# Products with the values as three float32r products of high and low parts, in one step of a hybrid GLA and attention backbone

## The chip, the cores and the metric

The kernel runs on one core of a Trainium2 chip, and the other cores are idle. A core has five engines, each with an instruction queue of its own that it works off in order: PE (TensorE, matrix products; the loading of its stationary operand is shown apart as PEld), DVE (VectorE), ACT (ScalarE), POOL (GpSimd) and SP (SyncE, which issues most transfers). They meet only through semaphores. SBUF is the on-chip memory; PE writes to PSUM, eight banks of 2 KB per partition, which DVE and ACT can read. The metric is the device time of one execution in microseconds; of several runs the median is given.

## The reference, cut to what matters

One inference step of two layers over 256 context tokens and 1024 latent tokens, model width 1024. Layer 0 mixes tokens with gated linear attention (GLA) of 4 heads, keys 128 wide and values 256 wide, scanned in both directions; layer 1 is grouped-query softmax attention. The change is in layer 0 alone:

```python
def step(S, inp):                       # one chunk of tokens, one head, one direction
    qi, ki, vi, gi = inp
    b = jnp.cumsum(gi, axis=2)
    b_last = b[:, :, -1:, :]
    qe = qi * jnp.exp(b)
    ke = ki * jnp.exp(-b)
    a = jnp.where(mask, jnp.einsum("bhtk,bhsk->bhts", qe, ke), 0.0)
    o = jnp.einsum("bhts,bhsv->bhtv", a, vi) + jnp.einsum("bhtk,bhkv->bhtv", qe, S)
    S = jnp.exp(b_last[:, :, 0, :])[..., None] * S + jnp.einsum(
        "bhsk,bhsv->bhkv", ki * jnp.exp(b_last - b), vi)
    return S, o
```

Two products have the values `vi` as an operand: the masked scores `a` times `vi` (the output inside a chunk), and the decayed keys transposed times `vi` (what a chunk adds to the state). All of it is in float32.

## The kernel before

The 1280 tokens are ten tiles of 128 (tiles 0 and 1 context, 2 to 9 latent). A start-up phase (to about 93 us) loads, normalises and modulates the tokens. Then comes the loop, `gla`, over five passes of ten tiles, 50 slots. In pass h (0 to 3) the tiles of head h go through decays, keys, scores and the scan in one direction; in pass h + 1 the other direction of head h is combined with it, scaled by its gate and stored. The fifth pass only combines. The same slots carry much other work as cover for each other: projections of the next heads (`mm3`, L247, each as three fp16 products of high and low halves), the splitting of attention weights into such halves (`split_ahead`, L329 and L330; `fill`, L308 and L309), and products with the conditioning vectors (L425). After the loop (about 540 us) follow the output projection of layer 0, the attention layer, and the last output projection.

In a slot, the parts that the change touches are these:

- `value_gate`: PE projects a tile's values into a PSUM bank (`mm`); ACT scales them into the SBUF tile `v` (L714, 128x256, three buffers).
- `intra`: PE transposes the decayed keys `en` of both directions into the bank `kt` (L781) and multiplies them with the queries `qe` into the other half of the bank (L784). DVE copies the transposed keys to `ks` (L787, 128x256) and masks the scores into `am` (L792); POOL adds the two directions to `at` (L793, 128x128).
- `outer`: PE multiplies `ks` with `v` for each direction into the bank `U` (L805 and L809), which ACT (L812) and DVE (L834) take into the scan; `scan` scales the state on POOL (L830, tiles `Sa`, `Sc`) and adds `U` on DVE (`Wa`, `Wc`).
- `local`: PE multiplies `at` with `v`, adds `qe` times the state in the same bank `A` (L851), and ACT copies it to `oa` (L854).

An fp32 product stands as one MATMUL in the program (it loads its own weights) and as two LDWEIGHTS and two MATMULs in the trace.

The order of the instructions on each engine is set when the kernel is built: a scheduler gives every instruction a priority in the order in which the code was written, shifted by the number that the table `LATER` has for the name of its `with self.later(name)` block (a higher number means later). Transfers from SP and ACT are set up by hardware; POOL's own (48 of them, most of them the attention outputs, L1408) use descriptors that POOL writes to a scratch in SBUF.

Of the kernel before, what the change touches and what calls it, by code (L numbers as in the profile page):

```python
# [9 lines left out]
F32 = mybir.dt.float32  # L10
I32 = mybir.dt.int32
AF = mybir.ActivationFunctionType
ALU = mybir.AluOpType
# [38 lines left out]
    "loc": -30,  # L52
    "kt": 30,
    "A": -110,
    "intra": -5,
    "ks": -90,
    "combine": -15,
    "cs": -40,
    "vg": -10,
    "u": 75,  # L60
    "gated": 50,
    "decay": -25,
    "outer": 10,
    "Uc": -100,
    "a9.qr": 30,
    "a.s1": 30,
    "gate": -5,
    "a0.key": -85,
    "x.qr": -40,
    "z.val": 35,  # L70
    "o": -155,
    "x.q": -15,
    "a0.qr": 15,
    "x.prep": -150,
    "oa": 30,
    "jobs": -20,
    "a.q": -210,
    "x.mod": -60,
    "x.res": -225,
    "a.val": 20,  # L80
    "a9.gate": 5,
    "a9.q": -200,
    "a.s0": -25,
    "a.qr": -200,
    "a9.s1": -160,
    "a0.s1": 390,
    "pieces8": 95,
    "filler": -30,
    "a0.s0": 75,
    "at": -115,  # L90
    "a0.rest": 30,
    "a0.gate": 65,
    "silu": -150,
    "a9.s0": -20,
    "x.setup": -150,
    "a9.val": 5,
    "combine9": 70,
    "jobs9": 220,
    "filler9": 15,
    "x.key8": 150,  # L100
    "eres": 110,
    "emod": -60,
    "wo2": 30,
    "fold": -30,
    "a0.q": 30,
    "wo3": 245,
    "x.key": -150,
    "s.v": 400,
    "s.q1": 60,
    "s.r0": -150,  # L110
    "s.n2": -55,
    "s.r1": 115,
    "gated9": 60,
    "eprep": 400,
    "x.kset": -30,
    "s.q0": -50,
    "s.s0": -140,
    "s.m1": -100,
    "s.s1": 220,
    "s.rk": 70,  # L120
    "s.n1": -100,
    "a9.val.3": -80,
    "a.s0.1": -15,
    "a9.val.1": -5,
    "a9.rest.0": 25,
    "a9.rest.2": -60,
    "a.rest.0": 100,
    "a.val.1": 25,
    "z.val.0": -100,
    "a.q.0": -110,  # L130
    "a9.qr.1": 60,
    "z.val.1": 165,
    "a9.gate.2": 85,
    "a9.s1.0": -200,
    "a9.q.0": -210,
    "a9.gate.0": -5,
    "a9.q.2": 30,
    "a9.s1.2": -135,
    "a.s0.3": -100,
    "a.s1.0": 55,  # L140
    "a9.gate.3": 15,
    "a9.s1.3": -150,
    "z.prep": -5,
    "a9.s0.0": -25,
}
# [15 lines left out]
class K:  # L161
# [545 lines left out]
    def value_gate(self, h, i, w):  # L707
        a, b = 0 if h < GH else DV, 2 * DV if h > 0 else DV
        ps = self.bank("mm")
        with self.later("vg"):  # L710
            self.tok_proj(i, [t[:, :, a:b] for t in w[0:2]], ps[:, a:b])
        if h < GH:
            v = self.t(self.tl, [P, DV], F32, "v", bufs=3)
            self.nc.scalar.activation(v, ps[:, 0:DV], AF.Copy, scale=self.inv_v[h])  # L714
            self.v[h][i] = v
        if h > 0:
            x = self.t(self.ew, [P, DV], F32, "gx", bufs=3)
            self.nc.scalar.activation(x, ps[:, DV:], AF.Copy, scale=self.inv_g[h - 1])  # L718
            with self.later("silu"):
                self.silu(x, DV)  # L720
            return x
# [49 lines left out]
    def intra(self, i, st):  # L771
# [13 lines left out]
        ks = self.t(self.ew, [P, 2, P], F32, "ks")  # L785
        with self.later("ks"):
            nc.vector.tensor_copy(ks, kt)  # L787
# [6 lines left out]
        st["at"], st["ks"] = at, ks  # L794


    def outer(self, h, i, a, st, prev, last):
# [5 lines left out]
        if needa:  # L803
            with self.later("Ua"):
                nc.tensor.matmul(ub[:, a, :], ks[:, a, :], v, start=True, stop=True)  # L805
        st["u"] = None
        if i < NTP or prev is not None:
            with self.later("Uc"):
                nc.tensor.matmul(ub[:, c, :], ks[:, c, :], v, start=True, stop=True)  # L809
# [33 lines left out]
    def local(self, h, i, a, st):  # L843
        nc = self.nc
        o = self.bank("A")[:, 0:DV]
        terms = [(st["at"], self.v[h][i])]
        if st["S"] is not None:
            terms.append((st["qe"][:, a, :], st["S"]))
        with self.later("local"):
            for j, (x, y) in enumerate(terms):  # L850
                nc.tensor.matmul(o, x, y, start=j == 0, stop=j == len(terms) - 1)  # L851
# [1103 lines left out]
```

## Time and profile before

| | |
|---|---|
| median of 3 runs | 1241.89 us (1240.9 to 1245.12) |
| profiled execution, span | 1240.9 us |
| PE busy | 1190.7 us (96%), 7990 MATMULs |
| DVE busy | 944.9 us (76%), 2177 instructions |
| ACT busy | 687.0 us (55%), 1694 instructions |
| POOL busy | 320.5 us (26%), 566 instructions |

The profiled execution is one run, and its own time is its span. A row of a group gives line, engine, operation, written tile, read tiles, shapes and count; then busy time, mean ns of one; then the idle time of the engine just before, and what ended it. A row of a line's own view gives minimum, median and maximum ns and the first and last start. A row of the timeline gives start, duration, engine, line and operation. A row of stages gives the stretch, its length, and for each engine busy us and (x instructions); then the granted clock of PE, the busy share of the DMA engines and GB/s.

### The profile page before, as it was taken

Reading aid. Unit: us, or ns where it says so; the run is one execution under the profiler, and the core shown is the slowest. Engines: PE = TensorE matmul, PEld = TensorE weight load, DVE = VectorE, ACT = ScalarE, POOL = GpSimd, SP = SyncE. Lnnn points to the kernel's source line nnn. Section 1 sums busy time; section 2 is a strip of 40 time slices with the busy share of each in tenths; the row PEclk is TensorE's granted clock in tenths of the full one; section 3 lists DMA queues with packets and bytes.
Section 4 is the critical chain, followed back from the end, with each engine's and each line's share of the span. In section 5 each row is a group of like instructions: output and inputs, shape, how many; then the busy total and the mean of one; then the engine's idle time right before and its main releaser. Section 6 shows DMA issues by size and latency. Waiting matters only on the chain. (4 is left out here: it accounts for less than half of the span.)

```text
span 1240.9 us, 22365 instructions
## 1 busy us (share of the span) xinstructions
PE 1190.7 (96%) x7990; PEld 778.3 (63%) x7990; DVE 944.9 (76%) x2177; ACT 687.0 (55%) x1694; POOL 320.5 (26%) x566
## 2 busy tenths in 40 slices
PE   5799999999999999799999999999999999989998
PEld 3467765655556566667776666776767666666444
DVE  4787779887888789976875787877767587786653
ACT  2565556665666657742333576666767676664110
POOL 0132122323321143311212443431322343311000
PEclk9999999999999999999999999999999999999999
DMA  9511566456555544489978787777958666979432
GB/s 378 196 69 73 196 202 228 127 185 203 175 191 164 189 132 161 112 186 307 204 174 203 178 163 138 132 145 133 199 124 161 124 118 132 205 139 246 158 137 85
DMA packets 318496, 210.14 MB, mean 169 GB/s; under 512 B 257158, under 2 KB 294702, under 8 KB 310064
## 3 DMA queue, kind: packets, MB, share of 16 engines
q1 hardware_dynamic: 311232, 191.18, 60.1%
q10 hardware_dynamic: 4688, 10.57, 2.2%
q0 software_dynamic: 2464, 6.95, 2.0%
q8 instruction: 63, 1.03, 0.3%
q14 instruction: 49, 0.40, 0.1%
HBM read 108.35 MB, written 38.96 MB: 119 GB/s over the span
## 5 line engine op out<-in xcount | busy, mean ns | idle before, releaser
L247 PEld LDWEIGHTS <-hT_hi 128*128 128x128 f16 x1920 | 187.6, 98 | 122.0 <-issue 5.6
L247 PE MATMUL mm<-whi,hT_hi 128*128 128x512 f16 (+1 forms) x576 | 200.2, 348 | 3.5 <-ACT gx L718 3.0
L247 PE MATMUL mm<-whi,hT_lo 128*128 128x512 f16 (+1 forms) x576 | 200.4, 348 | 0.0
L247 PE MATMUL mm<-wlo,hT_hi 128*128 128x512 f16 (+1 forms) x560 | 194.3, 347 | 0.7 <-DVE wlo L309 0.7
L247 PEld LDWEIGHTS <-whi 128*128 128x128 f16 x1232 | 120.3, 98 | 62.1 <-issue 2.2
L1344 PE MATMUL S<-kT,wst 128*128 128x512 f16 (+1 forms) x624 | 142.1, 341 | 4.1 <-ACT p L1352 4.0
L247 PE MATMUL mm<-hT_hi,whi 128*128 128x256 f16 (+1 forms) x480 | 141.1, 294 | 2.0 <-ACT gx L1392 2.0
L247 PE MATMUL mm<-hT_hi,wlo 128*128 128x256 f16 (+1 forms) x480 | 141.1, 294 | 0.0
L247 PE MATMUL mm<-hT_lo,whi 128*128 128x256 f16 (+1 forms) x480 | 141.1, 294 | 0.0
L1382 DVE SCALAR_TENSOR_TENSOR phl<-p,srec,phl 128x1280 f16<-128x1280 f32 (+1 forms) x79 | 105.3, 1332 | 40.6 <-ACT phl L1381 26.9
L247 PEld LDWEIGHTS <-hT_lo 128*128 128x128 f16 x960 | 94.1, 98 | 61.8 <-issue 1.1
L247 PE MATMUL mm<-PT,vh 128*128 128x256 f16 x672 | 114.6, 273 | 8.1 <-DMA PT<-phl 7.8
L1347 DVE TENSOR_REDUCE smx<-S 128x1 f32<-128x1280 f32 (+1 forms) x80 | 101.3, 1271 | 27.0 <-PE S L1344 26.9
L1352 ACT ACTIVATE p<-S,snb,acol 128x1280 f32<-128x1280 f32 (+1 forms) x80 | 99.1, 1239 | 12.5 <-DVE phl L1382 7.0
L1344 PEld LDWEIGHTS <-wst 128*128 128x128 f16 x624 | 61.4, 98 | 55.7 <-issue 6.9
L247 PE MATMUL mm<-PT,vl 128*128 128x256 f16 x336 | 91.6, 273 | 0.0
L1379 POOL TENSOR_SCALAR phl<-p,srec 128x1280 f16<-128x1280 f32 (+1 forms) x40 | 53.1, 1327 | 105.0 <-DVE srec L1370 57.1
L247 PEld LDWEIGHTS <-wlo 128*128 128x128 f16 x616 | 60.2, 98 | 29.2
L247 PEld LDWEIGHTS <-vh 128*128 128x128 f16 x672 | 65.1, 98 | 18.3 <-DMA PT<-phl 7.2
L1172 POOL TENSOR_TENSOR rope<-hx,ropet 128x64 f32<-128x64 f32 x160 | 51.2, 350 | 81.3 <-ACT hx L1308 63.8
L270 DVE TENSOR_REDUCE wmx<-wst 128x1 f32<-128x512 f32 x104 | 65.1, 677 | 3.5 <-DMA wst<-in_att_w 2.0
L238 POOL TENSOR_TENSOR hrs<-hrsa,mhalf 128x2 f32<-128x2 f32 x50 | 38.7, 775 | 106.8 <-DVE hrsa L236 106.5
(383 smaller groups left out, 2684.9 us busy)
## 6 DMA issues: line engine op xcount, KB each, us to landing
wada<-in_w_ada SPq DMA_DIRECT2D x16, 1024.0 KB, 5.4
wst<-in_att_w SPq DMA_DIRECT2D x14, 1024.0 KB, 5.3
wst<-in_gla_w_in SPq DMA_DIRECT2D x12, 1024.0 KB, 5.5
og_d<-og POOLq DMA_DIRECT2D x40, 128.0 KB, 2.8
wst<-og_d SPq DMA_DIRECT2D x5, 1024.0 KB, 6.0
og_d<-gx SPq DMA_DIRECT2D x37, 128.0 KB, 2.1
xr<-x_d SPq DMA_DIRECT2D x9, 512.0 KB, 3.3
out<-xr ACTq DMA_DIRECT2D x17, 256.0 KB, 2.0
```

Of the source, the lines that this page charges most:

```text
L238: nc.gpsimd.tensor_tensor(r, a, self.mhalf[:, 0:w], ALU.pow)
L247: self.pe = self.nc.tensor.matmul(out, a, b, start=k == 0 and j == 0, stop=k == n - 1 and j == 2).ins
L270: nc.vector.tensor_reduce(mx[:, j : j + 1], st[:, 2 * j : 2 * j + 2, :], AX.XY, ALU.max, apply_absolute_value=True)
L1172: nc.gpsimd.tensor_tensor(tv[:, h, :, w, :], xv[:, h, :, 1 - w, :], sn[:, :, w, :], ALU.mult)
L1344: nc.tensor.matmul(S[:, a : a + n], x, y, start=m == 0, stop=m == 2)
L1347: last = nc.vector.tensor_reduce(mx, S, AX.X, ALU.max).ins
L1352: nc.scalar.activation(p, S, AF.Exp, scale=self.sexp, bias=nb, accum_out=den)
L1379: nc.gpsimd.tensor_scalar(hi, p, r, 2.0 ** 14, ALU.mult, ALU.mult)
L1382: nc.vector.scalar_tensor_tensor(lo, p, r2, hi, ALU.mult, ALU.subtract)
```

## The change

`v`, the transposed keys and the masked scores are each kept as two float32r tiles: a high part, which is the value cast to float32r, and a low part, which is the value less its high part. A product with the values becomes three float32r products that add up in the same PSUM bank: high by high, high by low, low by high (`times_v`). The product of `qe` with the state stays one fp32 product. Per slot of passes 0 to 3 this adds on DVE the low part of `v` (`vlo`, 128x256) and the low part of the keys (`kl`, 128x256); the high part of the keys (`ks`) moves from a DVE copy to an ACT cast; ACT also gets the cast of `at` (128x128) and POOL its low part (128x128). The MATMULs written for these products go from 112 to 336. The scratch for POOL's descriptors shrinks from its default of 16384 bytes per partition to 4096. Nearly all numbers of `LATER` are new, and it has one new name, `vlo`.

```diff
+F32R = mybir.dt.float32r
 LATER = {
-    "kt": 30,
-    "A": -110,
-    "ks": -90,
+    "kt": 90,
+    "A": -265,
+    "ks": 110,
...
+    "vlo": 140,
 }
...
-            v = self.t(self.tl, [P, DV], F32, "v", bufs=3)
-            self.nc.scalar.activation(v, ps[:, 0:DV], AF.Copy, scale=self.inv_v[h])
-            self.v[h][i] = v
+            hi = self.t(self.tl, [P, DV], F32R, "v", bufs=3)
+            lo = self.t(self.tl, [P, DV], F32R, "vlo", bufs=3)
+            self.nc.scalar.activation(hi, ps[:, 0:DV], AF.Copy, scale=self.inv_v[h])
+            with self.later("vlo"):
+                self.nc.vector.scalar_tensor_tensor(
+                    lo, ps[:, 0:DV], self.inv_v[h], hi.bitcast(F32), ALU.mult, ALU.subtract
+                )
+            self.v[h][i] = hi, lo
...
-        ks = self.t(self.ew, [P, 2, P], F32, "ks")
+        ks = [self.t(self.ew, [P, 2, P], F32R, t) for t in ("ks", "kl")]
         with self.later("ks"):
-            nc.vector.tensor_copy(ks, kt)
+            nc.scalar.copy(ks[0], kt)
+            nc.vector.tensor_tensor(ks[1], kt, ks[0].bitcast(F32), ALU.subtract)
...
             nc.gpsimd.tensor_tensor(at, am[:, 0, :], am[:, 1, :], ALU.add)
-        st["at"], st["ks"] = at, ks
-
+            ah = [self.t(self.tl, [P, P], F32R, f"at{j}", bufs=2) for j in range(2)]
+            nc.scalar.copy(ah[0], at)
+            nc.gpsimd.tensor_tensor(ah[1], at, ah[0].bitcast(F32), ALU.subtract)
+        st["at"], st["ks"] = ah, ks
+
+
+    def times_v(self, out, x, v, stop=True):
+        for j, (a, b) in enumerate(((0, 0), (0, 1), (1, 0))):
+            self.nc.tensor.matmul(out, x[a], v[b], start=j == 0, stop=stop and j == 2)
...
-                nc.tensor.matmul(ub[:, a, :], ks[:, a, :], v, start=True, stop=True)
+                self.times_v(ub[:, a, :], [t[:, a, :] for t in ks], v)
...
-                nc.tensor.matmul(ub[:, c, :], ks[:, c, :], v, start=True, stop=True)
+                self.times_v(ub[:, c, :], [t[:, c, :] for t in ks], v)
...
-            for j, (x, y) in enumerate(terms):
-                nc.tensor.matmul(o, x, y, start=j == 0, stop=j == len(terms) - 1)
+            self.times_v(o, st["at"], self.v[h][i], S is None)
+            if S is not None:
+                nc.tensor.matmul(o, st["qe"][:, a, :], S, start=False, stop=True)
...
-    nc = _bacc.Bacc("TRN2", target_bir_lowering=False, num_devices=1)
+    nc = _bacc.Bacc("TRN2", target_bir_lowering=False, num_devices=1, dynamic_dma_scratch_size=4096)
```

How this moves instructions is shown at two places. Lines of the changed kernel are two higher near the top and up to fourteen higher at `local`. The first place is PE's queue in the third pass, at the products with the values of one tile; before:

```order
L851 MATMUL A_4316<-Sa_4312,qe_4082 128x256
L247 LDWEIGHTS whi_540_2369
L247 MATMUL mm_4321<-hT_lo_74,whi_540_2369 128x512
L805 MATMUL U_4307<-v_4124,ks_4218 128x256
L809 MATMUL U_4307<-v_4124,ks_4218 128x256
```

and in the changed kernel, where L810 is the line in `times_v`:

```order
L810 MATMUL U_4820<-v_4595,ks_4681 128x256
L810 MATMUL U_4820<-vlo_4596,ks_4681 128x256
L249 LDWEIGHTS whi_585_2521
L249 MATMUL mm_4844<-hT_lo_74,whi_585_2521 128x512
L249 LDWEIGHTS wlo_586_2522
L249 MATMUL mm_4844<-hT_hi_73,wlo_586_2522 128x512
L810 MATMUL U_4820<-v_4595,kl_4682 128x256
L810 MATMUL U_4820<-v_4595,ks_4681 128x256
L810 MATMUL U_4820<-vlo_4596,ks_4681 128x256
L810 MATMUL U_4820<-v_4595,kl_4682 128x256
```

The two products with the keys now are six MATMULs, with projection work between them where the low part `kl` is needed first; the local products (bank `A`) follow later. Between this tile's `kt` transposes and the first of these rows stand sixteen MATMULs 512 wide.

The second place is DVE's queue at the transposed keys, in the same pass; before:

```order
L834 TENSOR_TENSOR Wc_4739<-Sc_4737,u_665_2787 128x256
L822 COPY Wc_5101<-u_581_2507 128x256
L330 SCALAR_TENSOR_TENSOR split_4173<-wst_4046,p2s_4167,split_4173 128x512
L787 COPY ks_4218<-kt_4213 128x256
L792 COPY_PREDICATED am_37_150<-mask_146,kt_4213 128x256
```

and in the changed kernel:

```order
L212 TENSOR_REDUCE p2m_4783<-z_4781 128x1
L216 TENSOR_SCALAR p2c_4785<-p2m_4783 128x1
L719 SCALAR_TENSOR_TENSOR vlo_4745<-mm_4719,inv_v_996_4001,v_4744 128x256
L218 TENSOR_SCALAR p2e_4787<-p2c_4785 128x1
L795 TENSOR_TENSOR kl_4682<-kt_4676,ks_4681 128x256
L800 COPY_PREDICATED am_36_149<-mask_146,kt_4676 128x256
```

The copy of the keys is gone from DVE; in its place stands the subtraction for `kl`, which waits for ACT's cast to `ks`, ahead of the masking of the scores (`am`); and the low part of the next tile's values, `vlo`, stands shortly before it.

158 lines of the change are left out of this document (78 added, 80 removed).

## The prediction

> **What bounds the kernel now.** I read the stage table first: busy time by stretch, of the loop over heads and tiles (93 to about 465 us), of its last pass (465 to 540) and of the rest.
>
> ```profile
> span 1240.9 us, 22365 instructions
> ...
> core 0: us, PE busy (x) PEld busy (x) DVE busy (x) ACT busy (x) POOL busy (x), PEclk, DMA share, GB/s
> ...
> 186.00:279.00 93.00, 93.00 (x548) 55.73 (x545) 83.98 (x231) 60.65 (x159) 26.11 (x50) 1.00 0.55 180
> ...
> 93.00:465.00 372.00, 371.70 (x2302) 228.07 (x2300) 307.89 (x828) 224.37 (x586) 102.77 (x187) 1.00 0.53 172
> 465.00:540.00 75.00, 67.70 (x453) 47.86 (x452) 67.54 (x207) 53.81 (x142) 23.76 (x38) 0.98 0.52 148
> 540.00:1241.00 701.00, 681.83 (x4714) 460.34 (x4712) 506.07 (x996) 362.54 (x883) 176.37 (x308) 1.00 0.73 164
> ```
>
> In the loop PE is idle for 0.3 us of 372, at full clock (1.00). DVE has 83% on average and 90% between 186 and 279 us, ACT 60%, POOL 28%. But a busy PE need not be a full one, since the records of pipelined matmuls overlap. So I read the starts in the PE timeline, from one product to the next:
>
> ```profile
> 310.44 0.59 PE L805 MATMUL U<-v,ks 128*128 128x256 f32 x2
> 310.87 0.60 PE L809 MATMUL U<-v,ks 128*128 128x256 f32 x2
> 311.30 0.60 PE L851 MATMUL A<-v,at 128*128 128x256 f32 x2
> ...
> 385.70 0.27 PE L247 MATMUL mm<-hT_hi,wlo 128*128 128x256 f16 x1
> 385.81 0.27 PE L247 MATMUL mm<-hT_hi,whi 128*128 128x256 f16 x1
> ```
>
> Products follow each other without a gap (0.43, 0.43; 0.11): a full fp32 product of 128x256 is two MATMULs and takes 0.43 us, an fp16 MATMUL of the same width 0.11 us. The fp32 product costs four fp16 passes. A duration of 0.27 in such a row is mostly pipeline; the step of the starts is the price. So from 93 to 465 us PE sets the pace, and what is cut from its stream moves the end, as long as the others keep up.
>
> **The change: PE.** The products with the values are these:
>
> ```profile
> L805 PE MATMUL U<-v,ks x72: 377/380/484, 93.4 to 489.8; 128*128 128x256 f32 x72
> L809 PE MATMUL U<-v,ks x72: 378/379/483, 100.4 to 503.1; 128*128 128x256 f32 x72
> L851 PE MATMUL A<-v,at x80: 378/379/484, 94.7 to 504.2; 128*128 128x256 f32 x80
> ```
>
> At two MATMULs a product that is 36 + 36 + 40 = 112 products, 112 x 0.43 = 48.2 us of PE. Each becomes three float32r MATMULs of the same shape. No row shows float32r. The bounds are the two steps above: 0.11 us, if an operand whose low part has been taken out needs no splitting in the array, and 0.216 us (half of 0.43), if PE walks each 4-byte column twice as it does now. I take the lower, since the three terms (high by high, high by low, low by high) are those of the fp16 product of L247 and drop only low by low, so nothing is left for a second walk. A second price is the weight load: three fp32 loads a product in place of two. The loads' own records:
>
> ```profile
> 303.87 0.53 PEld L784 LDWEIGHTS kt<-qe,en 128*128 128x128 f32 x4
> 303.98 0.61 PE L784 MATMUL kt<-qe,en 128*128 128x128 f32 x4
> 304.43 0.27 PE L733 MATMUL z<-wa,r 98*128 98x256 f16 x1
> L784 PEld LDWEIGHTS kt<-qe,en x160: 187/192/247, 89.9 to 493.9; 128*128 128x128 f32 x160
> ```
>
> An fp32 load lasts 0.19 us, but four loads and MATMULs of 128 columns pass in 0.45 us, 0.112 each: loads overlap, and one per 0.112 us is possible. So a float32r product takes 3 x 0.109 = 0.327 to 3 x 0.112 = 0.336 us and saves 0.096 to 0.105. I take 0.10: 112 x 0.10 = **11.2 us** less PE (10.8 to 11.8).
>
> The Trainium skill, FP8 and Floating Point Precision, Matmul Precision, says that true fp32 is four passes and that the reduced-precision form reads four bytes and truncates them; by that a term is one pass and the sum is the one taken. The 0.43 us agree with four passes; of the reduced form no run here shows anything.
>
> **The change: DVE, ACT, POOL.** For each of 40 slots (a head and a tile) the copy of ks goes from DVE to ACT, DVE gains kl (PSUM minus SBUF) and vlo (PSUM times a column minus SBUF), ACT gains the cast of at, POOL gains the low part of at. The nearest rows, from 93 to 490 us:
>
> ```profile
> L764 DVE TENSOR_TENSOR en<-en,k 128x256 f32<-128x256 f32 x37 | 16.2, 440 | 1.8 <-ACT en L760 1.7
> L787 DVE COPY ks<-kt 128x256 f32<-128x256 f32 x38 | 15.8, 417 | 1.5 <-PE kt L784 1.5
> L743 DVE SCALAR_TENSOR_TENSOR g<-ls,g 128x256 f32<-128x256 f32 x36 | 15.3, 424 | 3.0 <-ACT ls L740 2.8
> L834 DVE TENSOR_TENSOR Wa<-Sa,U 128x256 f32<-128x256 f32 x31 | 12.8, 413 | 1.0 <-ACT u L812 0.6 <-POOL Sa L828 0.3
> L881 DVE SCALAR_TENSOR_TENSOR gx<-og,ors,gx 128x256 f32<-128x256 f32 x25 | 12.3, 493 | 0.3
> L854 ACT COPY oa<-A 128x256 f32<-128x256 f32 x38 | 14.0, 369 | 5.9 <-PE A L851 5.7
> L793 POOL TENSOR_TENSOR at<-am 128x128 f32<-128x128 f32 x38 | 22.1, 581 | 66.9 <-DVE am L792 46.8 <-DVE p2i L220 8.7 <-PE mm L247 4.3
> ...
> 486.74 0.41 DVE L834 TENSOR_TENSOR Wa<-Sa,U 128x256 f32<-128x256 f32 x1
> 487.07 0.41 DVE L748 TENSOR_TENSOR glo<-g,ghi 128x256 f16<-128x256 f32 x1
> 487.41 0.14 DVE L214 TENSOR_SCALAR p2c<-p2m 128x1 f32<-128x1 f32 x1
> ```
>
> kl at 0.41 replaces ks at 0.42: nothing. vlo is 0.33 (the step when DVE is full) to 0.49 (L881); I take 0.42 as L743 has it, 17 us over 40 slots. ACT gains 0.37 for ks and, for half of that width, 0.18 to 0.37 for at; at 0.28 that is 26 us in all. POOL gains 0.58 x 40 = 23 us. In the loop some 35 of the 40 slots lie before 465 us: DVE comes to 307.9 + 35 x 0.42 = 322.6 of about 361 us (89%), ACT to 224.4 + 35 x 0.65 = 247 (68%), POOL to 123 (34%). All fit under PE on average, so this work is hidden, except where DVE is nearly full:
>
> ```profile
> 186.00:279.00 93.00, 3.31 (x8) 1.00 0.55 180
> 465.00:540.00 75.00, 1.64 (x4) 0.98 0.52 148
> ...
> 480.00:495.00 15.00, 14.66 (x110) 11.68 (x108) 15.00 (x45) 10.55 (x33) 3.96 (x8) 1.00 0.62 211
> 510.00:525.00 15.00, 12.84 (x101) 10.15 (x100) 14.96 (x51) 11.40 (x33) 7.92 (x12) 1.00 0.39 101
> ```
>
> (The first two rows count the ks copies alone: 8 slots fall between 186 and 279 us, 4 behind 465.) From 186 to 279 DVE grows to 83.98 + 8 x 0.42 = 87.3, PE shrinks to 93 - 8 x 0.30 = 90.6. DVE at 96% delays PE at times: between 0 and 3.4 us (all of vlo on the path); I take 1.0. Behind 480 us DVE is full for 15 us and sets the pace itself: there three slots' vlo lie on the path, 3 x 0.37 = 1.1 us, and the four slots' PE saving, 4 x 0.30 = 1.2 us, isn't realised.
>
> POOL's extra work also touches DVE. L764 reads two SBUF tiles and means 0.44 us, L787 reads PSUM and means 0.417. With some seven instructions of the first kind a slot, 0.02 us each, POOL costs DVE about 0.15 us a slot now; 20% more POOL makes it 0.03 more, 1.2 us over the loop, off the path except where DVE is full, so inside the 1.0 taken. The Trainium skill, SBUF — State Buffer, Who interferes with whom, gives the mechanism: GpSimd and a VectorE instruction with two SBUF inputs lock one port pair against each other, and the loser waits. The rows agree in kind; vlo and kl, with one PSUM input, stay clear of it.
>
> The waits that are added: U's third product waits for kt, then ACT's ks, then DVE's kl, 0.37 + 0.41 us plus two queues, where one DVE copy stood. Behind the kt transposes shown in the order stand sixteen 512-wide MATMULs, each two 0.11 steps, before the first product: 16 x 0.22 = 3.5 us of cover. The at chain gets 0.28 + 0.58 us longer and its products stand later still. If ACT's queue holds ks up for over 2 us, PE stands at U, and the state Sa on POOL and Wa on DVE come late next; that is the first rival.
>
> **Keys and scratch.** The new keys shift work in the whole program but the counts outside the loop stay. Behind 540 us PE is idle for 701 - 682 = 19 us; a new order can win or lose a part of that. I take zero, within 4 us either way. A smaller scratch can only touch transfers that POOL issues itself, 48 in all, most of them these:
>
> ```profile
> L1408 POOL DMA_DIRECT2D og_d<-og x40 | 23.4, 584 | 86.2 <-DVE og L1407 59.1 <-DVE wm L1538 17.7 <-DVE srec L1372 3.4
> ```
>
> POOL had 86 us of idle time ahead of them, so a wait there of about a landing (2.8 us) would be hidden: zero; without that cover 40 x 2.8 us would be at stake, which nothing in the trace suggests.
>
> **Sum.** -11.2 + 1.2 + 1.1 + 1.0 = -7.9 us: 1240.9 becomes 1233.0 in the profiled execution. The median of the runs lies 1.0 above it, so **1234 us**, with 1229 to 1239 as this case's own range (terms at their bounds, keys within 4).
>
> **Rivals.** (1) *DVE or ACT paces the loop.* For it: DVE's 90% from 186 us, its 15.00 of 15 behind 480, and two more engine hops before U. Against: the 3.5 us of cover, and DVE's average of 89%. If about 0.25 us a slot stays on the path the gain is 1 to 2 us: 1240, within noise. It decides once the ks cast ends over 3 us behind kt. 13%.
>
> (2) *PE has room already.* The Trainium skill, Perfetto Trace Analysis, Identifying the Most-Contended Engine, judges TensorE's headroom by the busy share of weight loads, not of matmuls. Taken as a mechanism: loads fill 228 of 372 us, 61%, so PE would be waiting on something else for a third of the loop, and a cheaper product would buy nothing: 1242. The steps of 0.11 and 0.43 without a gap speak against it. 3%.
>
> (3) *Slower: float32r isn't a one-pass product.* If each term takes 0.216 us, a product takes 0.65, 0.22 more than now: 112 x 0.22 = +24, 1266 us. If the 0.19 us of a load are not overlapped, 0.57, +0.14 x 112 = +15.7, 1258 us. For it: fp32 rows now take two walks, and no row shows one. Against: the 0.112 step of fp32 loads. It decides from a step of 0.144 us (0.43/3). 8%.
>
> (4) *Slower: the new order loses more behind 540 us than the loop gains*, over 12 us of new PE waits, say PE standing for the transposed p tiles of attention: about 1247. Against: the counts there don't change, and idle was only 19 us. 5%.
>
> **How the numbers follow.** A measurement of this kernel tells 0.3%, 3.7 us, from no change. The forecast has 71%, and its range lies under 1238.2 but for a little: faster 0.71. Within 0.3% are (1), (2) and the edge: 0.16. Slower are (3) and (4): 0.13. The range 1227 to 1245 takes in the forecast and rivals (1) and (2) and leaves out (3), (4) and a gain that the keys bring besides.
>
> **What would show it.** Right: in the loop, three U rows at a step of 0.11 us; PE still idle-free from 93 us; the last pass beginning some 9 us earlier; DVE near 88 of 91 us in the stretch that was 186 to 279. Wrong: a step over 0.14 us at those rows; PE waits that name ks, kl, vlo or at for over 3 us in sum; PE idle behind the loop grown by over 5 us.

## The result, and the profile after

| | before | changed |
|---|---|---|
| median of 20 runs each, side by side | 1245.19 us | 1248.6 us (1243.15 to 1251.66) |
| profiled execution, span | 1240.9 us | 1248.9 us |
| PE busy | 1190.7 us | 1191.9 us |
| DVE, ACT, POOL busy | 944.9, 687.0, 320.5 us | 955.4, 705.3, 345.3 us |

The changed kernel takes 1.0023 times the time of the one before (95% interval 1.0013 to 1.0033): 2.9 us more, inside the 0.3% that counts as no change, where 7.9 us less had been forecast. The profiled execution of before took 1241.89 us, 3.3 less than its median here, that of the changed kernel 1250.68, 2.1 more than its own, so the 8.0 us between the spans overstate the difference.

The stage table of the changed kernel, with the columns of the prediction's:

```profile
span 1248.9 us, 22714 instructions
...
core 0: us, PE busy (x) PEld busy (x) DVE busy (x) ACT busy (x) POOL busy (x), PEclk, DMA share, GB/s
...
186.00:279.00 93.00, 91.16 (x569) 55.65 (x568) 81.62 (x232) 61.65 (x171) 32.23 (x59) 1.00 0.52 174
93.00:465.00 372.00, 366.90 (x2396) 226.78 (x2395) 314.51 (x857) 241.38 (x652) 115.77 (x221) 1.00 0.53 170
465.00:540.00 75.00, 66.56 (x445) 47.38 (x444) 67.98 (x210) 53.80 (x152) 30.61 (x46) 0.95 0.47 143
540.00:1249.00 709.00, 688.36 (x4759) 465.28 (x4756) 509.67 (x1005) 364.34 (x888) 181.96 (x309) 1.00 0.73 164
```

In the loop PE was idle for 0.3 us of 372 and is now idle for 5.1. DVE grew by 6.6 us, ACT by 17, POOL by 13. In the stretch from 186 to 279 us DVE has even less than before. Behind 540 us PE is idle for 20.6 us (19.2 before), so little changed there.

The new products, in the PE timeline and in the view of their line:

```profile
310.39 0.65 PE L879 MATMUL o<-Sc,qe 128*128 128x256 f32 x2
310.69 0.47 PE L810 MATMUL A<-v,at 128*128 128x256 f32 x1
311.00 0.28 PE L810 MATMUL A<-vlo,at 128*128 128x256 f32 x1
311.12 0.28 PE L810 MATMUL A<-v,at 128*128 128x256 f32 x1
311.24 0.59 PE L865 MATMUL A<-Sa,qe 128*128 128x256 f32 x2
```

```profile
L810 PEld LDWEIGHTS A<-v,at x80: 186/190/203, 98.3 to 506.6; 128*128 128x128 f32 x80
L810 PE MATMUL A<-v,at x80: 279/365/470, 98.3 to 506.8; 128*128 128x256 f32 x80
```

A float32r term is one load and one MATMUL, and the next one starts 0.12 us later (the record of the first begins early, while that of the product ahead of it still runs). The median step, over the 336 MATMULs and counted to the next other row, is 0.121 us: 0.363 a product, 0.069 less than the 0.432 of the fp32 product, 7.7 us in all. The loop still does not end earlier: the last local product starts at 506.8 us, and at 504.2 before. The output projection, which follows the loop, writes the bank `y`; its first product starts at 556.2 us, and at 549.5 before (first and last start stand behind the durations; the row of before, then that of the changed kernel):

```profile
L247 PE MATMUL y<-whi,hT_hi x128: 269/326/380, 549.5 to 671.4; 128*128 128x512 f16 x64, 128*128 128x256 f16 x64
L249 PE MATMUL y<-whi,hT_hi x128: 269/326/379, 556.2 to 678.6; 128*128 128x512 f16 x64, 128*128 128x256 f16 x64
```

So in this pair of traces 6.7 us are lost by the end of the loop and 1.3 behind it.

What takes the gain's place has to stand in the table of waits, 93 to 540 us (time in all, times, longest; the rows that bear on the change):

```profile
POOL at L804 <- ACT at L803: 23.8, 31, 2.5
ACT at L803 <- POOL at L801: 16.5, 13, 4.6
PEld L249 <- issue: 12.1, 20, 1.9
ACT gx L725 <- DVE vlo L719: 11.8, 12, 2.5
DVE wmx L272 <- DMA wst<-in_att_w: 8.4, 7, 2.6
PE mm L249 <- ACT gx L725: 5.0, 5, 1.8
PEld A L810 <- POOL at L804: 2.3, 4, 1.3
PEld U L810 <- DVE kl L795: 2.1, 3, 1.5
PEld U L810 <- ACT ks L794: 1.6, 3, 0.6
PE A L810 <- POOL at L804: 1.4, 2, 1.1
```

From the same table of before:

```profile
PEld L247 <- issue: 4.2, 4, 3.2
PE mm L247 <- ACT gx L718: 3.0, 1, 3.0
DVE wmx L270 <- DMA wst<-in_att_w: 2.0, 3, 0.9
```

PE now stands at the products for the low part of the keys, for that of the masked scores, and for the cast of the keys. ACT stands 12 times behind DVE: `gx` (L725, the gate's half of the projection bank) waits for `vlo` (L719), which reads the other half of that bank. PE in turn waits for `gx` before it writes such a bank again (`mm`, 5 times instead of once). But `vlo` is not shown to be the reason: in the kernel without low parts, further down, PE has that wait 5 times as well (4.8 us). No data passes between `vlo` and `gx`; both only read. The Trainium skill, PSUM — Partial Sum Buffer, PSUM bank collisions raise a hardware error, gives a reason for such a wait: ScalarE and VectorE may not access the same bank and quadrant at once, even to read, and software has to keep them apart. That this is why the wait stands in this program is not shown by any run here. The prediction did not see it: it took `vlo` as 0.42 us on DVE and nothing else.

The new instructions themselves are about as dear as estimated (ns, minimum, median, maximum):

```profile
L719 DVE SCALAR_TENSOR_TENSOR vlo<-mm,inv_v,v x37: 468/475/486, 103.7 to 490.2; 128x256 fp32r<-128x256 f32 x37
L795 DVE TENSOR_TENSOR kl<-kt,ks x40: 406/416/426, 94.1 to 501.0; 128x256 fp32r<-128x256 f32 x40
L794 ACT CAST ks<-kt x40: 349/372/388, 93.7 to 500.4; 128x256 fp32r<-128x256 f32 x40
L803 ACT CAST at<-at x40: 280/298/349, 96.0 to 504.3; 128x128 fp32r<-128x128 f32 x40
L804 POOL TENSOR_TENSOR at<-at,at x40: 452/458/1492, 96.4 to 504.7; 128x128 fp32r<-128x128 f32 x40
```

(The row of `vlo` has 37 of its 40, since the view begins at 93 us and three lie ahead of it.)

### The profile page after: what moved, and what is told of

The parts are those of the page before. It is cut to its first block, busy times and chain, and to the rows that moved or that the text cites. A ratio compares the mean times of both kernels' runs of the same rounds, so it can differ in the third digit from the quotient of the medians.

```text
span 1248.9 us, 22714 instructions
## 1 busy us (share of the span) xinstructions
PE 1191.9 (95%) x8102; PEld 781.2 (63%) x8102; DVE 955.4 (76%) x2217; ACT 705.3 (56%) x1774; POOL 345.3 (28%) x606
## 4 chain that ended last, share of the span: by engine, by line
PE 58%; DVE 15%; DMA 14%; ACT 4%; issue 2%; POOL 2%; SPq 0%; ACTq 0%; POOLq 0%; DVEq 0%
PE mm L249 31%; PE y L249 12%; PE S L1358 6%; DMA PT<-phl 4%; PE kv L249 3%; DMA wst<-in_att_w 2%; DVE wmx L272 1%; DVE split L332 1%; PE U L810 1%; DMA hT_lo<-split 1%; DMA wst<-og_d 1%; DMA wst<-in_gla_w_in 1%; DVE smx L1361 1%; DVE phl L1396 1%; PE mm L427 1%
## 5 line engine op out<-in xcount | busy, mean ns | idle before, releaser
L1186 POOL TENSOR_TENSOR rope<-hx,ropet 128x64 f32<-128x64 f32 x160 | 53.8, 367 | 77.1 <-ACT hx L1322 62.6
```

The source lines that it names most:

```text
L1186: nc.gpsimd.tensor_tensor(tv[:, h, :, w, :], xv[:, h, :, 1 - w, :], sn[:, :, w, :], ALU.mult)
```

## Experiments: the keys and the scratch

Every ratio below is against runs of the kernel before on the same chip, with its 95% interval. First the parts of the change that touch no product.

The scratch alone, in the kernel before:

```diff
-    nc = _bacc.Bacc("TRN2", target_bir_lowering=False, num_devices=1)
+    nc = _bacc.Bacc("TRN2", target_bir_lowering=False, num_devices=1, dynamic_dma_scratch_size=4096)
```

> The kernel before with the smaller scratch for POOL's descriptors and nothing else. Theories A and B: no change, within 2 us of before. Theory C (POOL waits for room in the scratch): 3 us or more slower, with longer POOL rows at the attention outputs.

Measured: 0.9993 (0.9979 to 1.0008): no effect that can be told from none.

The new keys alone, in the kernel before (the whole `LATER` of the changed kernel, all else old):

```diff
-    "ks": -90,
+    "ks": 110,
...
```

> The kernel before with the changed kernel's order keys and nothing else. Theory A (the splitting work on ACT, DVE and POOL gives the PE saving back): the keys alone move the time by no more than 4 us either way, 1241 to 1249. Theory B (the new keys lose time, mostly behind the loop): 6 to 12 us slower than before, and first S tile later by as much.

Measured: 1.0137 (1.0117 to 1.0156), 17 us slower, more than either theory had.

The changed kernel with the old keys:

```diff
-    "ks": 110,
+    "ks": -90,
...
-    "vlo": 140,
```

(A name that the table lacks counts as zero.)

> The changed kernel with the order keys of before (vlo at zero). Theory A: the splitting work costs as much in any order, so within 5 us of the changed kernel or slower, 1246 to 1256. Theory B: 6 to 12 us faster than the changed kernel, so faster than before, 1237 to 1243.

Measured: 1.0122 (1.0105 to 1.0138). With old keys on old products at 1 and new keys on new products at 1.0023, either half alone loses 15 to 17 us. So each set of keys fits its own program, and the effects of keys and products do not add up. The step "keys: zero, within 4 us either way" had the wrong form: it was a term of a sum.

## Experiments: prices changed under a new order

Each of these edits the changed kernel and leaves the keys as they are. The scheduler models times, so a changed price also moves instructions: in the traces some 1600 to 2050 of DVE's 2217 instructions stand in stretches of the same order as in the changed kernel, and some 1270 to 1670 of ACT's 1774. That limits what this group can tell.

PE dearer: one fp32 product of the high parts in place of the three.

```diff
-        for j, (a, b) in enumerate(((0, 0), (0, 1), (1, 0))):
-            self.nc.tensor.matmul(out, x[a], v[b], start=j == 0, stop=stop and j == 2)
+        self.nc.tensor.matmul(out, x[0].bitcast(F32), v[0].bitcast(F32), start=True, stop=stop)
```

> The changed kernel with each product with the values as one full fp32 product of the two high parts: the casts and low parts are still computed on ACT, DVE and POOL but the low parts are not multiplied, so the output lacks them. PE is back at 0.43 us a product, from the 0.36 that the changed trace shows (three steps of 0.121). If PE sets the pace (theory A as a toll on top of PE): 112 x 0.07 = 7.7 us slower than the changed kernel, about 1256. If the splitting work on the other engines sets the pace: equal to the changed kernel within 2 us.

Measured: 1.0107 (1.009 to 1.0124), some 10 us over the changed kernel, as if PE set the pace, but in a new order.

PE cheaper: high and low parts in bf16, in all three pairs of tiles.

```diff
-            hi = self.t(self.tl, [P, DV], F32R, "v", bufs=3)
-            lo = self.t(self.tl, [P, DV], F32R, "vlo", bufs=3)
+            hi = self.t(self.tl, [P, DV], BF16, "v", bufs=3)
+            lo = self.t(self.tl, [P, DV], BF16, "vlo", bufs=3)
...
```

> The changed kernel with the high and low parts kept as bfloat16 and not as float32r; same instructions on every engine, but the parts hold 16 bits together, so the products are less exact than the reference's. Theory A3 (the float32r product itself costs more than a one-pass product, 0.121 us a step for its 4-byte weight load and not 0.109): steps of 0.109, 336 x 0.012 = 4 us less PE, 3 to 5 us under the changed kernel. If the step is not what costs: within 2 us.

Measured: 1.0042 (1.0025 to 1.0058), slower than the changed kernel by 2.4 us where 3 to 5 us less had been expected if the step costs. Its timeline shows the products at the step that the prediction took for float32r:

```profile
310.80 0.27 PE L810 MATMUL A<-v,at 128*128 128x256 bf16 x1
310.91 0.27 PE L810 MATMUL A<-vlo,at 128*128 128x256 bf16 x1
311.02 0.27 PE L810 MATMUL A<-v,at 128*128 128x256 bf16 x1
```

and the view of their line a shorter load:

```profile
L810 PEld LDWEIGHTS <-at x120: 95/98/147, 97.2 to 508.8; 128*128 128x128 bf16 x120
```

PE much cheaper: only the product of the high parts, the low parts still made.

```diff
-        for j, (a, b) in enumerate(((0, 0), (0, 1), (1, 0))):
-            self.nc.tensor.matmul(out, x[a], v[b], start=j == 0, stop=stop and j == 2)
+        self.nc.tensor.matmul(out, x[0], v[0], start=True, stop=stop)
```

> The changed kernel with the high by high term alone: the low parts are still computed but no MATMUL uses them, so the output lacks both cross terms. PE has 224 MATMULs at 0.121 us less, 27 us. Theory P (PE still sets the pace of the loop): about 1222, 24 to 27 us under the changed kernel. Theory D (the splitting work, most of all DVE's, has become the pace): 0 to 8 us under it, 1240 to 1249.

Measured: 1.0049 (1.003 to 1.0069). PE's 27 us less bought nothing, and by this run alone PE would not set the pace at all. The same program in a held order, below, is faster.

The low parts left out one at a time, with the instruction that makes them; the terms that used them take the high part instead:

```diff
-            lo = self.t(self.tl, [P, DV], F32R, "vlo", bufs=3)
+            lo = hi
...
```

> The changed kernel without the instruction vlo: the second term takes the high part of v again, so the output lacks the low part of v. PE's work is unchanged, DVE has 40 x 0.475 = 19 us less, and gx no longer waits for it. Theory D: 7 to 15 us under the changed kernel, 1234 to 1242. Theory P: within 2 us of it.

Measured: 1.0012 (0.9994 to 1.0031).

```diff
-        ks = [self.t(self.ew, [P, 2, P], F32R, t) for t in ("ks", "kl")]
+        ks = [self.t(self.ew, [P, 2, P], F32R, "ks")]
...
-            nc.vector.tensor_tensor(ks[1], kt, ks[0].bitcast(F32), ALU.subtract)
+            ks = [ks[0], ks[0]]
```

> The changed kernel without the instruction kl: the third term of U takes ks again, so the output lacks the low part of the keys. DVE has 40 x 0.416 = 16.6 us less, and DVE's masking of the scores no longer stands behind a wait for ACT. Theory D: 6 to 13 us under the changed kernel. Theory P: within 2 us. If it gains clearly more than the run without vlo, it is the wait for ACT's cast and not DVE's load that costs.

Measured: 1.0062 (1.0039 to 1.0085). Less work, more time, against either theory.

```diff
-            nc.gpsimd.tensor_tensor(ah[1], at, ah[0].bitcast(F32), ALU.subtract)
+            ah = [ah[0], ah[0]]
```

> The changed kernel without the low part of at: the third term of the local product takes the high part again, so the output lacks it. POOL has 40 x 0.46 = 18 us less and no longer waits for ACT's cast (23.8 us). If the at chain is what PE waits for: 4 to 7 us under the changed kernel. Theory D: within 2 us of it.

Measured: 1.0034 (1.0015 to 1.0054).

None of the three gains what a theory of a loss at that place had forecast. Next, single waits are taken away. `gx` is written ahead of `vlo`, so that it no longer waits for it:

```diff
+        if h > 0:
+            x = self.t(self.ew, [P, DV], F32, "gx", bufs=3)
+            self.nc.scalar.activation(x, ps[:, DV:], AF.Copy, scale=self.inv_g[h - 1])
+        if h < GH:
             with self.later("vlo"):
...
-            x = self.t(self.ew, [P, DV], F32, "gx", bufs=3)
-            self.nc.scalar.activation(x, ps[:, DV:], AF.Copy, scale=self.inv_g[h - 1])
```

> The changed kernel with one statement moved: the ACT copy of the gate gx out of the bank mm is written ahead of the DVE instruction vlo, which reads the same bank, so that gx no longer waits for vlo (11.8 us of ACT in the changed trace, and PE then waits 5.0 us for gx). Theory A1 (this wait gives the saving back): the wait is gone and the time is 4 to 7 us under the changed kernel, 1242 to 1246. Theory A2 (the loss lies in the chain at, its cast on ACT, its low part on POOL): within 2 us of the changed kernel. Either way the keys were not set for this order, which may add some us.

Measured: 1.0017 (1.0 to 1.0034). The wait of `gx` for `vlo` is gone from its trace, the time is that of the changed kernel. So that wait, conspicuous as it is, isn't shown to cost anything; a new order could hide what it costs.

The cast of the masked scores on POOL, so that the chain from `am` to the low part stays on one engine:

```diff
-            nc.scalar.copy(ah[0], at)
+            nc.gpsimd.tensor_scalar(ah[0], at, 1.0, 1.0, ALU.mult, ALU.mult)
```

> The changed kernel with the high part of at made on POOL and not on ACT, so that the sum, its high part and its low part follow each other on POOL. Theory A2: ACT's 16.5 us of waiting for at and POOL's 23.8 us of waiting for ACT go, and the time is 4 to 7 us under the changed kernel. Theory A1: within 2 us of it, or slower by POOL's 40 x 0.46 = 18 us more work.

Measured: 1.0027 (1.0011 to 1.0043): no gain. The two edits together:

> Both moves together. If the two waits are what the saving was lost to, 8 to 10 us under the changed kernel, 1238 to 1241, faster than before; if neither is, within 3 us of the changed kernel.

Measured: 1.0018 (1.0004 to 1.0032). Ten kernels around the changed one, with up to 27 us taken from PE or up to 19 from DVE, lie between 1.0012 and 1.0122, and none is clearly faster than it. Either nothing here is on the path, or every edit pays a toll for its order.

## Experiments: prices changed with every order held

To tell these apart, the following kernels are built twice. The first build only gives the order of the instructions on each of the five engines; the second has the edit, and an issue-order edge from each instruction to the next on its engine holds that order. No kernel was run with its order held and nothing else changed. But the traces show that holding adds no instruction: apart from the products themselves, PE's 7766 MATMULs follow each other exactly as in the kernel whose order was taken, and the other engines' instructions differ only by those that the edit adds, takes away or changes.

```diff
+                for seq in order.values():
+                    for p, q in zip(seq, seq[1:]):
+                        tc.add_manual_dep(traced[q], traced[p].name, dep, reason="order of the first build")
```

**In the order of before.** The three operands are written as float32r by the instructions that write them anyway, and the product is one float32r product:

```diff
-            v = self.t(self.tl, [P, DV], F32, "v", bufs=3)
+            v = self.t(self.tl, [P, DV], F32R if FINAL else F32, "v", bufs=3)
-        ks = self.t(self.ew, [P, 2, P], F32, "ks")
+        ks = self.t(self.ew, [P, 2, P], F32R if FINAL else F32, "ks")
-        at = self.t(self.tl, [P, P], F32, "at", bufs=2)
+        at = self.t(self.tl, [P, P], F32R if FINAL else F32, "at", bufs=2)
```

> The kernel before with every engine's instructions held in exactly its own order (issue-order edges between neighbours). The tiles of the values, of the transposed keys and of the masked scores are written as float32r by the instructions that write them now, and each of the 112 products is one float32r product of them: no low parts, so two of three terms are left out, and no instruction is added. PE loses 112 x (0.432 - 0.12) = 35 us, nothing else changes. If PE sets the pace in the loop in this order: 20 to 31 us faster than before (DVE would then have some 308 of 341 us), about 1215 to 1225. If PE was as busy as it was only because the other engines and the weights left it just enough work: within 5 us of before, about 1240 to 1245.

Measured: 0.9904 (0.9878 to 0.993), 12 us faster (9 to 15). Neither expectation was met: what is cut from PE does move the end, but by about a third of the cut.

```profile
93.00:465.00 372.00, 359.80 (x2250) 209.42 (x2250) 317.27 (x860) 231.88 (x612) 109.49 (x196) 1.00 0.55 176
```

PE is now idle for 12.2 us of the 372, and no other engine is full (DVE has 85%), so a chain through several queues probably paces it now; the table doesn't say which.

The same with each product written three times, so that PE has the MATMULs of the changed kernel:

```diff
+    def again(self, out, x, v):
+        if FINAL:
+            for _ in range(2):
+                ADDED.append(self.nc.tensor.matmul(out, x, v, start=True, stop=True).ins.name)
```

> As the one-term kernel in the order of before, but each product is written three times over (each time anew, so that the last one counts): PE does just as many float32r MATMULs as the changed kernel, no engine does anything else than before, and the order is that of before. 112 x (0.432 - 0.363) = 7.7 us less PE. If PE sets the pace: 6 to 8 us faster, about 1237 to 1239. If it does not: 1243 to 1246. Dearer than before only if a float32r MATMUL costs more in a stream than the 0.12 us read from the trace of the changed kernel.

Measured: 0.9911 (0.9887 to 0.9935), 11.1 us faster (8.1 to 14.1). That is more than either expectation and more than the 7.7 us less on PE, and close to the forecast's own term of 11.2 us. By whole times, the one-term kernel with its 27 us less on PE is only 1 us faster than this one. The traces divide the time otherwise, as told under the table further down.

```profile
93.00:465.00 372.00, 369.10 (x2413) 229.13 (x2412) 308.91 (x834) 226.42 (x590) 106.66 (x189) 1.00 0.54 172
```

The whole work of the changed kernel, with the instructions that both kernels share held in the order of before and the new ones put in where they come ready:

```diff
-            nc.vector.tensor_tensor(ks[1], kt, ks[0].bitcast(F32), ALU.subtract)
+            self.new(lambda: nc.vector.tensor_tensor(ks[1], kt, ks[0].bitcast(F32), ALU.subtract))
...
+    def new(self, f):
+        if FINAL:
+            ADDED.append(f().ins.name)
```

> The whole computation of the changed kernel, with every instruction that both kernels share held in the order of before on its engine; only the new ones (low parts, casts, second and third terms; the copy of the keys goes from DVE to ACT) are put in between where they come ready by the planner's model. If the split's work fits in under PE and the loss lies in the orders: 3 to 8 us faster than before, 1237 to 1242. If the split's work costs more than the cheaper products give: 3 to 15 us slower than before, 1248 to 1260, as the changed kernel with the old keys (1.2% slower).

Measured: 1.0228 (1.0202 to 1.0254), 28 us slower than before and 39 slower than the three-product kernel, more than expected. In its trace PE stands 9.1 us (9 times) for ACT's cast of the scores and 10.0 us (5 times) for `gx`, 93 to 540 us. The split's work does not fit into an order that was made without it.

**In the order of the changed kernel.** Two of the three terms left out, low parts still made:

```diff
+            if FINAL and j:
+                continue
```

> The changed kernel with every engine held in exactly its order and two of the three terms of each product left out (the low parts are still made): 224 MATMULs, 27 us of PE, less and nothing else. If the changed kernel lost its gain because PE no longer sets the pace there: within 4 us of the changed kernel, 1244 to 1249. If PE still sets the pace and the one-term kernel tried before lost its gain to its new order: 15 to 27 us faster than the changed kernel, 1221 to 1234.

Measured: 0.9982 (0.9966 to 0.9998), 0.41% or 5.1 us (2.7 to 7.5) under the changed kernel, for 27 us less on PE: between the expectations, nearer the first.

```profile
93.00:465.00 372.00, 356.31 (x2228) 205.50 (x2225) 322.28 (x877) 246.03 (x671) 121.24 (x227) 1.00 0.55 175
```

It is the program of the one-term kernel above (1.0049) in another order: the toll of planning anew, with keys fitted to something else, was 0.67%, 8 us. That is as much as most of the effects which that group was looking for.

No low parts, each product three times with the high parts:

```diff
+    def low(self, f):
+        if not FINAL:
+            GONE.append(f().ins.name)
...
-            self.nc.tensor.matmul(out, x[a], v[b], start=j == 0, stop=stop and j == 2)
+            if FINAL:
+                self.nc.tensor.matmul(out, x[0], v[0], start=True, stop=stop or j < 2)
+                continue
```

> The changed kernel, every engine held in exactly its order, without the three low parts (of the values and the keys on DVE, 80 instructions and 36 us; of the masked scores on POOL, 40 instructions and 18 us). Each product is written three times with the high parts (each time anew, so that the last one counts), so PE has the same MATMULs. The copy of the keys and the cast of the masked scores stay on ACT. If the low parts keep the cheaper products from paying: 8 to 14 us faster than the changed kernel, at 1234 to 1240, where the three-product kernel in the old order is. If the moves to ACT or the new order itself ate the gain: 1243 to 1249.

Measured: 0.997 (0.9951 to 0.9989), with runs from 1237.13 to 1246.54 us: 6.6 us (3.9 to 9.3) under the changed kernel, between the two expectations, and 7.3 (3.5 to 11.1) over the three-product kernel in the old order. Against before it is 3.7 us (1.4 to 6.1) faster.

The low parts made, but not used by PE:

```diff
+            if FINAL:
+                self.nc.tensor.matmul(out, x[0], v[0], start=True, stop=stop or j < 2)
+                continue
```

> As the kernel without low parts, in the order of the changed kernel, but the low parts are made and not used: each product is written three times with the high parts. DVE and POOL do all the work of the changed kernel, and PE waits for no low part. If the engines' time for the low parts is what costs: as the changed kernel, 1244 to 1249. If PE standing for the low parts (some 9 us of PE stalls at the products in the trace) is what costs: 5 to 9 us faster than the changed kernel, 1239 to 1243, and little slower than without low parts.

Measured: 0.9995 (0.9978 to 1.0013), 3.5 us (0.9 to 6.1) under the changed kernel, between the two expectations. The waits of this kernel, 93 to 540 us, still hold that of `gx` for `vlo`, and none of PE for a low part:

```profile
POOL at L807 <- ACT at L806: 24.2, 31, 2.7
ACT gx L728 <- DVE vlo L722: 11.9, 12, 2.4
PE mm L252 <- ACT gx L728: 6.1, 6, 2.4
PEld U L814 <- ACT ks L797: 1.6, 3, 0.6
```

## Where the gain went

Against the median of before (1245.4 us), by the ratios; the intervals of two kernels are added in quadrature:

| step | ratio | us from the step ahead |
|---|---|---|
| cheaper products, old order | 0.9911 | -11.1 (-14.1 to -8.1) |
| new order; cast of the keys and of the scores on ACT | 0.9970 | +7.3 (3.5 to 11.1) |
| low parts made, not used | 0.9995 | +3.1 (-0.1 to 6.3) |
| low parts used: the changed kernel | 1.0023 | +3.5 (0.9 to 6.1) |

The sum is +2.8 us. These are whole executions. The traces, one execution each, tell where in the program the time goes; the loop's end is marked by the first product of the output projection (us):

| kernel | loop's end | from there to the end |
|---|---|---|
| before | 549.5 | 691.4 |
| before with the small scratch, same order | 550.0 | 693.4 |
| one term, old order | 537.6 | 691.4 |
| cheaper products, old order | 546.8 | 687.1 |
| no low parts, new order | 545.4 | 691.2 |
| low parts made, not used | 554.1 | 693.7 |
| the changed kernel | 556.2 | 692.7 |

The one-term kernel wins its 12 us in the loop. The three-product kernel wins 2.7 us there and 4.3 behind it, where PE does the same work in the same order as before. So its 11.1 us can't all be put down to the cheaper products: in the loop the trace shows less than the 7.7 us taken from PE, not more. Nor do the traces show the second step: the loop without low parts ends no later than that of the three-product kernel. A single trace is only so good for this: that of the kernel without low parts is of an execution 5 us under its median, that of the next kernel 4.7 over it. The low parts are a loss by either measure: 6.6 us by the ratios, 10.8 at the loop's end.

The last step has a witness in the trace. From the starts in the PE timeline, less the usual step of the row ahead, a MATMUL of these products costs on average, with the standing before it, 130 ns in the three-product kernel in the old order, 137 without low parts, 142 with low parts unused, and 152 in the changed kernel (median 120 to 122 ns in all). From 142 to 152 ns are 3.3 us over 336 MATMULs. At 152 ns the new products cost 51 us, as much as the 224 fp32 MATMULs at 227 ns: in the changed kernel PE has its cheaper products and stands beside them for what they save.

The trace also shows what PE stands for. From the masking of the scores to their last part the median is 0.6 us before (POOL's sum alone) and 2.1 in the changed kernel (sum, cast, low part). The first local product starts 2.7 us behind that part before, and 1.4 in the changed kernel; in 12 of 40 slots it has less than 0.3 us, in place of 1 slot. The keys are no later for their way through ACT: the cast `ks` ends 0.8 us behind the scores' product in the bank `kt`, where the copy on DVE ended 1.7 us behind it; their low part `kl` ends 2.6 us behind it.

The second step is not taken apart. Two waits of PE are longer in the kernel without low parts than in the three-product kernel in the old order: `mm` for `gx`, 4.8 us in 5 waits against 3.2 in one, and the loads' waits that end in "issue" (no reason in the trace), 11.7 against 4.4. The order of the changed kernel has the casts on ACT built in, so whether the extra hop, ACT's 26 us or the order itself costs the 7 us, and whether they are lost in the loop, stays open. The third step can't be told from nothing by its own interval; together with the fourth it can (3.9 to 9.3).

## Why the prediction was wrong, by its steps

- *PE sets the pace in the loop, and what is cut from its stream moves the end.* Right in direction, not in size: in the order of before, 35 us cut brought 12. By whole times the first 7.7 us brought 11 and the next 27 only 1, as if PE had a lead of some 11 us over the next chain of waits; by the loop's ends in the traces the 7.7 us brought 2.7 and the 35 brought 11.9, as if a third of any cut came out. Which of the two holds stays open. The condition "as long as the others keep up" was judged by shares of busy time (DVE 89%, ACT 68%). Such shares do not show how close the next chain is: the one-term kernel left PE idle for 12 us with DVE at 85%.
- *112 x 0.10 = 11.2 us.* Too large by the trace's steps: a term takes 0.121 us, not 0.109 to 0.112, so a product saves 0.069 us and all of them 7.7. (float32r loads take 190 ns like those of fp32, bf16 loads 98; the two only go together.) That the three-product kernel measured 11.1 is luck as far as this sum goes: the steps don't explain it, and in its trace 4.3 us were won behind the loop. The 7.7 lies just outside the interval of the measurement. The rival of a dearer float32r (from a step of 0.144 us) is out: 0.121 us.
- *The new work fits under PE, so it is hidden.* This is the step that failed: the low parts were put at nothing in the loop but for the stretches where DVE is full. Making and using them costs 6.6 us (3.9 to 9.3), in one and the same order. Without them the changed kernel is 3.7 us faster than before, with them 2.9 slower, so they turn the gain into none. The instructions had about the expected length (0.475, 0.416, 0.372, 0.298, 0.458 us). What was missed is that others stand behind them. PE standing for the low parts is measured: 3.5 us (0.9 to 6.1), and 3.3 in the trace. The prediction had named PE waits for `ks`, `kl`, `vlo` or `at` of over 3 us as a sign of being wrong; the view of L810 has 10.3 us of them, matmuls and loads together. ACT's `gx` behind `vlo` and POOL behind ACT behind POOL at the masked scores are long in the table of waits. Taking either away gained nothing, but in a new order, so their share of the rest is not shown.
- *3.5 us of cover before the first product with the keys.* That the loads of PE wait only 1.6 to 2.1 us for `ks` and for `kl` each agrees with it. The larger wait, `at` through ACT back to POOL, was passed over with "later still".
- *Losses of +1.2, +1.1 and +1.0 us where DVE is full.* From 186 to 279 us DVE is at 81.62 of 93 us, 5.7 below the 87.3 forecast; that the new keys spread the work is likely, but not tested. The 1.1 us also take `vlo` at 0.37 us, where the rest of the working takes 0.42.
- *Keys: zero within 4 us.* Alone they cost 17 us, and with the new products they save 12 to 13 of what the old ones would lose: not a term of a sum.
- *Scratch: zero.* Right (0.9993). *Nothing behind the loop*: right within 1.3 us (691.4 and 692.7 us), which also rules out the fourth rival.
- *The rivals.* The first, in which part of each slot's gain stays on the path and the result is no change, came nearest. Its number, 0.25 us a slot, would be 0.35 if all of the 13.9 us lost behind the cheaper products were put down to 40 slots. Its condition, a cast of the keys that ends over 3 us behind `kt`, holds in 7 of 40 slots, and the copy of before was as late in 10: by that hop alone it did not come true. The second, that PE has room already, is wrong for the 12 us that the one-term kernel won and right for the other 23 that were cut there. The Trainium skill, Perfetto Trace Analysis, Identifying the Most-Contended Engine, judges TensorE's headroom by MFU (the share of its peak rate that the matmuls reach) and the busy share of weight loads; by the loads' 61% alone PE would have had room, and the 12 us (1.0%) won speak against reading that as room for all of a cut.

No full computation tried here beats the kernel before. The one-term and three-product kernels in the old order do, by 1%, but they leave out the low parts.

## What to carry to other kernels

An engine that is busy for 100% need not give back all that is cut from its stream: here 35 us less gave 12. Measure that first, by making the work cheaper and leaving out what the cheapness will cost; then add the cost, here 160 new instructions and their hops between engines, one part at a time. When a scheduler with fitted keys sets the order, hold the order on every engine before comparing prices, or the toll of a new order (here 8 to 17 us) hides the effect. And look in the traces where in the program a difference lies: whole times and the loop's end did not agree here.

## What the runs showed of the hardware

- A float32r MATMUL of 128x256 shows as one load and one MATMUL, where fp32 shows two of each. If float32r is the reduced-precision form of the Trainium skill, FP8 and Floating Point Precision, Matmul Precision, which reads four bytes and truncates them, where true fp32 takes four passes, the trace agrees. It does not quite have the price of a 16-bit MATMUL: 0.121 us from start to start with a load of 190 ns, against 0.11 us and 98 ns for bf16 in the same place. That the load is the cause is a guess; the two only go together.
- The three-product kernel ran faster by more than its steps account for (11.1 against 7.7 us), though the loop in its trace ended only 2.7 us earlier; why is open.
